# The ends of a stage, one transfer over two queues, and another order of feed-forward products in a two-layer encoder

## The chip, the core and the metric

The kernel runs on one core of a Trainium2 chip. The core has a matrix engine (PE, with its weight loader PEld), a vector engine (DVE), a scalar engine (ACT), a general engine (POOL), a queue for synchronisation and transfers (SP), and 16 DMA engines that all queues share. The metric is device time in microseconds of one execution. Before the change, three runs took 915.63, 916.13 and 916.91 us; the median is 916.13 us.

## The reference

The input x has 256 tokens of width 1024, in float32. Two layers follow, each made of a feed-forward part, an attention part and a second feed-forward part, and one last norm:

```python
for l in range(DEPTH):                                   # 2
    x = x + 0.5 * swiglu(rms_norm(x, n1[l]), wg1, wu1, wd1)   # hidden width 2816
    h = rms_norm(x, nm[l]); q, k, v = split(h @ w_in[l])
    out_a = windowed_gqa_sink(...)                       # 8 heads, window of 128
    out_b = differential_attention(...)                  # 4 heads, norm per head
    x = x + concat(out_a, out_b) @ w_out[l]
    x = x + 0.5 * swiglu(rms_norm(x, n2[l]), wg2, wu2, wd2)
return rms_norm(x, nf)

def swiglu(h, wg, wu, wd): return (silu(h @ wg) * (h @ wu)) @ wd
```

So there are four feed-forward parts; the text calls them parts 1 to 4, in order of time. Attention stands between parts 1 and 2 and between parts 3 and 4; part 3 follows part 2 directly.

## The kernel before

**Products.** Every float32 operand is split into a high part (a rounded copy, made by ACT) and a low part (the rest, made by DVE with a subtraction). A product of two matrices then takes three PE products: high with high, low with high, high with low. The 256 tokens are two blocks of 128; PE holds a block of x and streams 512 columns of weights. A feed-forward part takes its 2816 hidden columns in groups 0 to 4 of 512 and a last group of 256.

**Weights.** A step's weights are 1 MB, which come by DMA into one of six `raw` buffers (SP issues it), and are split in two halves into `w` buffers: for each half a cast on ACT and a subtraction on DVE. There are 14 `w` buffers, seven halves, so the splits run some three steps ahead of PE (`weights`, `ahead`, `emit_split`). A half's buffers are free again when PE has used it.

**The order of a part.** `order()` holds a list of names, which is worked off from left to right. Instructions keep the program's order on PE, ACT, DVE and POOL within a feed-forward part, so the list sets the order on each of them, and the order of the weights' transfers too. The names:

- `Pgp` is a quarter of an ordinary group g: p = 0, 1 are the two halves of the gate product, 2, 3 those of the up product; 24 PE products each (4 slices of x, 2 blocks, 3 products). After p = 1 ACT makes two silus, after p = 3 DVE makes the hidden values.
- Groups 2 and 4 are computed with seven half-size products instead of eight, by Strassen's way of adding operands first. `Sga`, `Sgd`, `Sgab`, `Sgc`, `Sgabc`, `Sgbc`, `Sgabcd` are these seven, 12 PE products each. The letters say which quarters of the weights have been added up. Sums are made by POOL with an accumulating DMA ("gather": b onto a, d onto a, c onto b) or by DVE ("plus": c onto a). Between them results are added up in bank `acc` and in `tmp` buffers: S2abc, S2bc and S2abcd all add into one PSUM bank, and DVE must have read it before the next of them starts.
- `x1` makes one of the four summed operands of x that the seven products need: DVE adds, ACT casts, DVE subtracts (`make_sums`).
- `F` turns the hidden values of a group: DVE transposes small blocks and SP issues four moves that put them in place (`Blocks`, `Flip`). `T` makes their high and low parts, on ACT and DVE. `Dgh` is the down product of group g for half h of the output columns, 24 products.
- `L0`, `L1` are the last group of 256; its turned values are `T5`. `A` stands for extra work: in part 1 the constants of attention (a small PE transpose, some small DVE work, one ACT exponential), in part 4 the final gain's load.

Part 1 to 4 all begin with 96 products of group 0, whose second half of slices needs x's second half. After the list come the last products of the part (`ffn_end`). They are: group 4's down products for output half 0; the tail (the last group's down product, which needs T5); group 3's remaining half (`late`); and output half 1.

**The end of parts 1 to 3** is `ffn_close`. For output half 0 it makes group 4's products of token block 0 (12), the tail of block 0 (6), adds the sum to x and, on DVE, transposes the new x (`closed`, `flip`), and then does the same for block 1. When both blocks are there, `flip` calls `move`, and SP issues four DMAs that finish turning x for the next stage; `flipped` makes x's operands from it. Output half 1 is turned in the same way at the end of part 2 and at the end of both attention parts (in `mix`). `Residual.late` makes those operands when the next stage has begun.

Of the kernel before, what the change touches and what calls it, by code (L numbers as in the profile page):

```python
# [32 lines left out]

def order():

    names = """P10 x1 S2a S2d x1 P11 x1 P12 T0 P13 x1 S2ab D00 S2c D01 S2abc P30 F1 S2bc P31 S2abcd T1 S4a P32 D10 P33 S4d T2 S4ab L0 F3 S4c D20 S4abc D21 T3 S4bc D11 S4abcd L1 D30 T4 T5 A"""
    out = []
    for n in names.split():
        what, g, rest = n[0], n[1:2], n[2:]
        if what == "x":  # L40
            out.append(("sums", 0, int(g)))
        elif what == "S":
            out.append(("seven", int(g), rest))
        elif what == "P":
            out.append(("plain", int(g), (int(rest) // 2, int(rest) % 2 * 4)))
        elif what == "D":
            out.append(("down", int(g), int(rest)))
        elif what == "L":
            out.append(("last", 0, int(g) * 4))
        elif what == "T":  # L50
            out.append(("turned", int(g), 0))
        elif what == "F":
            out.append(("flip", int(g), 0))
        elif what == "A":
            out.append(("aside", 0, 0))
    return out


ORDER = order()
GATHER = {"a": "b", "abc": "d"}  # L60
HELD = ("c", "abc")
# [3 lines left out]
def trunk(ctx: ExitStack, tc: tile.TileContext, x, n1, g1, u1, d1, nm, w_in, sink,  # L65
          lq1, lk1, lq2, lk2, subln, w_out, n2, g2, u2, d2, nf, out):
    nc = tc.nc
    sp = nc.sync
# [18 lines left out]
    pe, act, dve, pool = Kept(nc.tensor), Kept(nc.scalar), Kept(nc.vector), Kept(nc.gpsimd)  # L87
# [157 lines left out]
    def ahead(n):  # L245

        n = min(n, 2 * len(specs) - 1)
        while True:
            if at["split"] <= n and at["prep"] > at["split"] // 2:
                for _ in emit_split(*divmod(at["split"], 2)):  # L250
                    pass
                at["split"] += 1
            elif at["prep"] <= min(n // 2 + 1, len(specs) - 1) and at["dma"] > at["prep"] and \
                    (specs[at["prep"]].prep is None or at["split"] >= 2 * at["prep"]):
                prep = specs[at["prep"]].prep or []
                for todo in prep if isinstance(prep, list) else [prep]:
                    todo()
                at["prep"] += 1
            elif at["dma"] < min(at["use"] + AHEAD, len(specs)) and (specs[at["dma"]].moves is None or len(raws) < N_RAW):
                if specs[at["dma"]].moves is not None:  # L260
                    for _ in emit_dma(at["dma"]):
                        pass
                at["dma"] += 1
            else:
                break

    def weights(less=0, held=False):

        i = at["use"]
        at["use"] += 1  # L270
        if i > 1:
            ahead(2 * i + HALVES - less)
        w = loaded[i]
        w.held = held
        return w
# [58 lines left out]
    class Blocks:  # L334
# [7 lines left out]
            sq = self.sq.rearrange("p (g t m) -> p t g m", g=4, t=2)[:, t]  # L342
            dve.transpose(sq, src.rearrange("p (c i g) -> p g c i", i=32, g=4))

        def move(self):
            to = self.back.rearrange("p (b m) -> p b m", b=4)
            if not self.by_block:
                to = self.back.rearrange("p (t b m) -> p b t m", t=2, b=4)
            for b in range(4):
                sp.dma_start(to[:, b], self.sq[32 * b:32 * b + 32])  # L350

        def turned(self):
            if not self.by_block:
# [6 lines left out]
    class Norm:  # L360
# [21 lines left out]
        def flip(self, h, t):  # L382

            if h not in self.flips:
                self.flips[h] = Blocks(by_block=False)
            self.flips[h].take(xk[:, t, h * 512:h * 512 + 512], t)
            if t:
                self.flips[h].move()

        def flipped(self, h, js=(0, 1)):  # L390
            sl = self.flips[h].turned()
# [240 lines left out]
    class Residual:  # L632
# [14 lines left out]
        def late(self, k):  # L647

            if k == 1:
                if 1 in self.nxt.flips:  # L650
                    self.nxt.flipped(1)
                else:
                    self.nxt.pair(2)
                    self.nxt.pair(3)
                self.squares(1)
            elif k == 2:
                self.nxt.stats()
                self.nxt.copies()
# [180 lines left out]
    def ffn_end(parts, last):  # L839

        accs, hT, rest, late = parts
        hT = [None] * (2 * (NGRP - 1)) + hT
        hE = []
        w = {0: weights()}

        def group(h, order, a=None, c=slice(None), first=0):
            tokens(a or accs[h], hT, w[h], G4, first=first, last=last[h], order=order, cols=c)

        def tail(h, order=BY_TOKENS, a=None, c=slice(None)):
            if not hE:  # L850
                hE.extend(rest)
            tokens(a or accs[h], [None] * (2 * NGRP) + hE, w["rest"], 4 * NGRP, last=last[h], order=order, cols=c, h=h)

        return group, tail, late, w

    def ffn_close(parts, nxt, flips):
        group, tail, late, w = ffn_end(parts, (FC - 1, G4 + 3))
        res = Residual(nxt, parts[0])

        def closed(h, t):  # L860
            res.add(h, t)
            if h in flips:
                nxt.flip(h, t)

        group(0, [(k, 0) for k in range(4)])
        w["rest"] = weights()
        tail(0, [(k, 0) for k in range(2)])
        closed(0, 0)
        group(0, [(k, 1) for k in range(4)])
        tail(0, [(k, 1) for k in range(2)])  # L870
        closed(0, 1)
        late()
        w[1] = weights(2)
        tail(1)
        nxt.flipped(0)
        group(1, [(k, 0) for k in range(4)])
        ahead(2 * at["use"] - 2 + HALVES)
        closed(1, 0)
        group(1, [(k, 1) for k in range(4)])
        closed(1, 1)  # L880
        res.squares(0)
        nxt.late = res.late
# [242 lines left out]
    for l in range(DEPTH):  # L1125
        final = l == DEPTH - 1
        parts = ffn(norm, attention_constants, take_x) if l == 0 else ffn(norm)
        norm_m = Norm(16 + l * 8, False)
        ffn_close(parts, norm_m, (0,))
        norm2 = Norm(32 + l * 8)  # L1130
        mix(l, norm_m, norm2)
        parts = ffn(norm2, final_gain if final else None, final=final)
        if not final:
            norm = Norm((l + 1) * 8)
            ffn_close(parts, norm, (0, 1))
# [23 lines left out]
    group, tail, late, w = ffn_end(parts, ((FC - 1), FC - 1))  # L1159
# [50 lines left out]
```

## Time and profile before

One profiled execution took 918.63 us; its span is 916.8 us, at a mean granted clock of 0.998.

| | |
|---|---|
| median of three runs | 916.13 us |
| profiled execution, its span | 918.63 us, 916.8 us |
| PE busy | 899.1 us, 98% |
| DVE busy | 728.3 us, 79% |
| ACT busy | 559.0 us, 61% |
| bytes moved by DMA | 209.26 MB, mean 228 GB/s |
| DMA engines' share, first 7 of 40 slices | 90% or more |

How to read it: a timeline row has its start in us, its length in us, the engine, the operation, what it writes and reads (names without buffer numbers), the count of instructions merged in it, and in brackets how long the engine stood idle before it and what released it. `ps` is PSUM, `raw` and `w` are weights before and after splitting, `s` is a general buffer, `q` and `v` on PE rows are the summed operands. Queued work of SP and POOL has rows of its own (SPq is an issue, not the transfer). PE's products are pipelined, so that the end of a row overlaps the next.

### The profile page before, as it was taken

What the parts mean: (1) busy time and instruction counts of PE and PEld (TensorE: products, weight loads), DVE (VectorE), ACT (ScalarE), POOL (GpSimd) and SP (SyncE); (2) the same over time, 40 slices, a digit from 0 to 9 for tenths busy, and PEclk for the clock granted to TensorE, in tenths of its full rate; (3) what the DMA queues carried; (4) which work ended last, traced back from release to release, by engine and by line L of the source; (5) the groups of instructions that cost most, each with busy time, mean ns of one, the idle gap of its engine ahead of it and who ended that gap; (6) DMA issues with size and microseconds to landing.
All of it is one profiled execution on the core that took longest, in us unless ns stands there. A gap on an engine that the chain in (4) does not pass through costs nothing.

```text
span 916.8 us, 12682 instructions
## 1 busy us (share of the span) xinstructions
PE 899.1 (98%) x4540; PEld 756.2 (82%) x4540; DVE 728.3 (79%) x1098; ACT 559.0 (61%) x917; POOL 52.0 (6%) x73
## 2 busy tenths in 40 slices
PE   8999999999999999999999999999999999999997
PEld 6888788799888888888788888878997888888886
DVE  6687898779966788898668987977798668987982
ACT  6766566467754766666366665645676466665652
POOL 0400010000000000010000100000000000100001
PEclk9999999999999999999999999999999999999999
DMA  9999999666425779999669799996653449799931
GB/s 337 307 264 283 312 232 347 191 186 184 137 91 161 215 214 312 292 247 349 179 197 292 195 289 287 279 343 186 170 169 101 136 136 273 193 286 297 288 123 46
DMA packets 131247, 209.26 MB, mean 228 GB/s; under 512 B 5486, under 2 KB 51632, under 8 KB 131184
## 3 DMA queue, kind: packets, MB, share of 16 engines
q1 hardware_dynamic: 117168, 181.96, 59.6%
q0 software_dynamic: 12928, 25.46, 16.3%
q10 hardware_dynamic: 1088, 1.05, 0.3%
q8 instruction: 35, 0.57, 0.3%
q14 instruction: 28, 0.23, 0.1%
HBM read 192.71 MB, written 1.05 MB: 211 GB/s over the span
## 4 chain that ended last, share of the span: by engine, by line
PE 87%; DMA 5%; DVE 3%; issue 2%; ACT 0%; SPq 0%; POOL 0%; POOLq 0%; ACTq 0%; DVEq 0%
PE ps L80 87%; DVE s L80 2%; DMA s<-s 2%; DMA raw<-in_ffn_w_gate_dram 1%; DVE w L80 1%; DMA raw<-in_ffn_w_up_dram 1%; DMA raw<-in_w_in_dram 1%; DMA xk<-in_x_dram 0%; SPq L350 0%; ACT w L80 0%; POOL raw L80 0%; ACT s L80 0%; ACT tmp L80 0%; DVE ra L80 0%; DVE xk L80 0%
## 5 line engine op out<-in xcount | busy, mean ns | idle before, releaser
L80 PE MATMUL ps<-w,s 128*128 128x512 f32 (+1 forms) x2994 | 689.1, 390 | 5.1 <-ACT s L80 3.7
L80 PEld LDWEIGHTS ps<-w,s 128*128 128x128 f32 x2994 | 559.8, 188 | 122.8 <-ACT s L80 5.0
L80 DVE TENSOR_TENSOR w<-raw,w 128x1024 fp32r<-128x1024 f32 (+1 forms) x416 | 435.0, 1086 | 87.1 <-ACT w L80 83.0
L80 ACT CAST w<-raw 128x1024 fp32r<-128x1024 f32 (+1 forms) x416 | 375.1, 943 | 182.2 <-PE ps L80 114.3
L80 PE MATMUL ps<-s,w 128*128 128x256 f32 x672 | 84.0, 285 | 0.0
L80 PEld LDWEIGHTS ps<-s,w 128*128 128x128 f32 x672 | 81.7, 192 | 1.1
L80 PE MATMUL ps<-w,q 128*128 128x512 f32 x288 | 69.2, 389 | 0.0
L80 PEld LDWEIGHTS ps<-w,q 128*128 128x128 f32 x288 | 54.1, 188 | 11.2
L80 DVE STREAM_TRANSPOSE s<-s 128x512 f32<-128x512 f32 (+1 forms) x48 | 46.4, 1006 | 0.0
L80 DVE TENSOR_TENSOR s<-s,s 128x256 fp32r<-128x256 f32 x88 | 31.5, 419 | 15.0 <-ACT s L80 14.9
L80 ACT CAST s<-s 128x256 fp32r<-128x256 f32 x88 | 29.3, 402 | 14.8 <-DMA s<-s 14.8
L80 ACT ACTIVATE s<-s,negm 128x256 f32<-128x256 f32 x64 | 31.9, 500 | 8.7 <-DVE negm L80 8.7
L80 ACT ACTIVATE s<-s,gcol 128x256 fp32r<-128x256 f32 (+1 forms) x40 | 17.0, 500 | 31.6 <-DMA s<-s 31.6
L80 POOL DMA_DIRECT2D raw<-in_ffn_w_up_dram x16 | 20.7, 1297 | 256.9 <-DVE w L80 130.0
L80 ACT ACTIVATE tmp<-ps,r 128x512 f32<-128x512 f32 (+1 forms) x40 | 24.8, 643 | 12.4 <-PE ps L80 11.9
L80 ACT CAST q<-tmp 128x512 fp32r<-128x512 f32 x20 | 12.3, 616 | 28.5 <-DVE tmp L80 28.5
L80 DVE SCALAR_TENSOR_TENSOR s<-s,gcol,s 128x256 fp32r<-128x256 f32 x24 | 10.1, 483 | 20.7 <-ACT s L80 20.7
L80 PE MATMUL ps<-w,v 128*128 128x512 f32 x96 | 23.1, 389 | 0.0
L80 POOL TENSOR_TENSOR r<-ms,mhalf 128x2 f32<-128x2 f32 x6 | 4.3, 710 | 302.4 <-DVE ms L80 302.4
L80 PEld LDWEIGHTS ps<-w,v 128*128 128x128 f32 x96 | 18.0, 188 | 3.7
L80 DVE SCALAR_TENSOR_TENSOR s<-ps,hr,tmp 128x512 f32<-128x512 f32 (+1 forms) x32 | 20.4, 676 | 0.0
L80 DVE TENSOR_TENSOR q<-tmp,q 128x512 fp32r<-128x512 f32 x20 | 13.8, 689 | 8.3 <-ACT q L80 8.3
(112 smaller groups left out, 430.4 us busy)
## 6 DMA issues: line engine op xcount, KB each, us to landing
raw<-in_ffn_w_down_dram SPq DMA_DIRECT2D x44, 1024.0 KB, 9.0
raw<-in_ffn_w_gate_dram SPq DMA_DIRECT2D x39, 1024.0 KB, 6.2
raw<-in_ffn_w_up_dram SPq DMA_DIRECT2D x39, 1024.0 KB, 7.9
raw<-in_ffn_w_up_dram POOLq DMA_DIRECT2D x16, 1024.0 KB, 9.4
raw<-in_w_in_dram SPq DMA_DIRECT2D x14, 1024.0 KB, 7.7
s<-s SPq DMA_DIRECT2D x104, 128.0 KB, 4.7
raw<-in_ffn_w_gate_dram POOLq DMA_DIRECT2D x8, 1024.0 KB, 10.0
raw<-in_ffn_w_gate_dram SPq DMA_DIRECT2D x8, 512.0 KB, 4.4
```

What stands on the lines that cost most here:

```text
L80: ins = issue(*a, **k)
```

## The change

Three things are changed.

1. In `ffn_close`, group 4's products of both blocks for output half 0 come first, 24 in a row. Then come the tail of block 0, its closing, the tail of block 1, its closing.
2. `move` takes a list of queues and deals its four DMAs to them in turn. x's second half is moved by SP and ACT, two DMAs each; its first half and all hidden groups by SP alone as before.
3. The list in `order()` is another. S2a stands before P10. T0 stands before P11 and the fourth x1 before P12. S2c follows S2ab directly, D00 comes after it, D01 after S2bc. F1 comes later. In the second half S4ab, S4c and S4abc follow one another. T3 comes later, and A stands between T4 and T5. The steps themselves are the same.

```diff
-    names = """P10 x1 S2a S2d x1 P11 x1 P12 T0 P13 x1 S2ab D00 S2c D01 S2abc P30 F1 S2bc P31 S2abcd T1 S4a P32 D10 P33 S4d T2 S4ab L0 F3 S4c D20 S4abc D21 T3 S4bc D11 S4abcd L1 D30 T4 T5 A"""
+    names = """S2a x1 P10 x1 S2d x1 T0 P11 x1 P12 P13 S2ab S2c D00 S2abc P30 S2bc D01 P31 F1 S2abcd S4a P32 T1 P33 T2 D10 F3 S4d D20 S4ab S4c S4abc L0 S4bc D21 D11 T3 S4abcd L1 D30 T4 A T5"""
...
-        def move(self):
+        def move(self, queues=(sp,)):
...
-                sp.dma_start(to[:, b], self.sq[32 * b:32 * b + 32])
+                queues[b % len(queues)].dma_start(to[:, b], self.sq[32 * b:32 * b + 32])
...
-                self.flips[h].move()
+                self.flips[h].move((sp, act) if h else (sp,))
...
-        group(0, [(k, 0) for k in range(4)])
+        group(0, [(k, t) for t in range(2) for k in range(4)])
         w["rest"] = weights()
-        tail(0, [(k, 0) for k in range(2)])
-        closed(0, 0)
-        group(0, [(k, 1) for k in range(4)])
-        tail(0, [(k, 1) for k in range(2)])
-        closed(0, 1)
+        for t in range(2):
+            tail(0, [(k, t) for k in range(2)])
+            closed(0, t)
         late()
```

## The prediction

> **What bounds the kernel now.** I read the page's busy shares first, then the timeline of PE alone for the places where its row of products breaks off, then the timeline of all engines around those places, then DVE's timeline in the first third of a feed-forward part, because DVE prepares the weights of every product.
>
> ```profile
> PE 899.1 (98%) x4540; PEld 756.2 (82%) x4540; DVE 728.3 (79%) x1098; ACT 559.0 (61%) x917; POOL 52.0 (6%) x73
> ```
>
> PE is busy 98% of the span, and the granted clock of the run is 0.998. No product is added or taken away, so the change can only act on the breaks in PE's row. These are the ones it can touch:
>
> ```profile
> 83.26 2.88 PE L80 MATMUL ps<-w,q 128*128 128x512 f32 x12
> 85.98 5.60 PE L80 MATMUL ps<-w,s 128*128 128x512 f32 x24
> 93.07 24.73 PE L80 MATMUL ps<-w,s 128*128 128x512 f32 x108 [1.48 <-DVE tmp L80]
> ...
> 144.84 19.20 PE L80 MATMUL ps<-w,s 128*128 128x512 f32 x84
> ...
> 164.45 3.25 PE L80 MATMUL ps<-w,s 128*128 128x512 f32 x12 [0.24 <-ACT s L80]
> 168.21 19.61 PE L80 MATMUL ps<-w,s 128*128 128x512 f32 x84 [0.51 <-ACT s L80]
> ...
> 418.84 21.92 PE L80 MATMUL ps<-w,s 128*128 128x512 f32 x96
> 442.56 68.60 PE L80 MATMUL ps<-w,s 128*128 128x512 f32 x300 [1.79 <-ACT s L80]
> ...
> 595.32 21.98 PE L80 MATMUL ps<-w,s 128*128 128x512 f32 x96
> 618.41 19.61 PE L80 MATMUL ps<-w,s 128*128 128x512 f32 x84 [1.12 <-ACT s L80]
> ```
>
> Twelve products run from 83.26 to 85.98: 2.72 us, 0.2267 us for one. With that rate a break is start to start less the products between. At 168.21 PE lost 168.21 - 164.45 - 12 x 0.2267 = 1.04 us; at 442.56 it lost 442.56 - 418.84 - 96 x 0.2267 = 1.96; at 618.41, 1.33; at 93.07, 93.07 - 85.98 - 24 x 0.2267 = 1.65. The first three are the ends of parts 1, 2 and 3: PE stands before the tail, whose operands (T5) come last by a move through DMA. The fourth is in part 1: S2abcd waits for DVE to read S2bc's bank.
>
> **Stage ends.** At each end the 12 products of group 4 with block 1 now stand before the tail: 12 x 0.2267 = 2.72 us of work, for breaks of 1.04, 1.96 and 1.33. A second short wait comes right behind each, since the tail's second product needs the low part:
>
> ```profile
> 443.01 7.17 PEld L80 LDWEIGHTS ps<-w,s 128*128 128x128 f32 x32 [0.27 <-DVE s L80]
> ```
>
> With 0.27 each the needs are 1.31, 2.23 and 1.60, all under 2.72; the cover is left with 0.5 at the tightest. Gain 5.1. If a landing came 0.5 us later than now, part 2 would give the excess back.
>
> ```profile
> 625.10 0.68 DVE L80 TENSOR_TENSOR xk<-xk,ps 128x512 f32<-128x512 f32 x1
> 625.81 1.09 DVE L80 STREAM_TRANSPOSE s<-xk 128x512 f32<-128x512 f32 x1
> ...
> 633.93 1.71 ACT L80 ACTIVATE s<-s,gcol 128x256 fp32r<-128x256 f32 x4 [3.20 <-DMA s<-s]
> ...
> 637.86 3.04 PE L80 MATMUL ps<-s,w 128*128 128x256 f32 x24
> ```
>
> What is late next is x's first half, here at the end of part 3. Its block 0 is added and transposed only 6 products (1.36 us) before block 1, where it was 18 before. One add and one transpose take 625.81 - 625.10 = 0.71 and about 1.0, 1.7 us, so block 1 starts some 0.35 late and so do its four moves. The operands made from them begin at 633.93 and PE uses them at 637.86, so 0.35 costs nothing there. In part 1 the constants' work on DVE now stands ahead of T5's low parts:
>
> ```profile
> 168.87 0.19 DVE L80 COPY gcol<-ps 128x34 f32<-128x34 f32 x1
> ...
> 171.99 3.48 DVE L80 TENSOR_TENSOR w<-raw,w 128x1024 fp32r<-128x1024 f32 x3
> ```
>
> That is 3.1 us, which can begin once group 4's low parts are made, about 166; PE wants T5's at 164.45 + 5.44 = 169.9. It just fits, and I keep that end's 1.3 us as uncertain.
>
> **x's second half over two queues.** SP issues four moves one behind the other:
>
> ```profile
> 290.29 2.67 SPq L350 DMA_DIRECT2D s<-s  x4
> ...
> 295.20 1.71 ACT L80 ACTIVATE s<-s,gcol 128x256 fp32r<-128x256 f32 x4 [7.01 <-DMA s<-s]
> ...
> 290.30:291.30 1.00, 1.00 (x6) 0.82 (x5) 1.00 (x1) 0.00 (x0) 0.00 (x0) 1.00 0.00 0
> ...
> 290.30:295.30 5.00, 5.00 (x23) 4.13 (x22) 1.02 (x1) 0.10 (x1) 0.00 (x0) 1.00 0.53 105
> ```
>
> (The last two rows are stretches of 1 and of 5 us; their last but one figure is the DMA engines' share.) PE has no break here, so nothing is gained at the place itself. But ACT stood 7.01 us for the landing, and from there it works without a break up to the part's first gates, so parts 2, 3 and 4 start that much earlier on ACT and DVE. How much: two issues fewer in a row are 2 x 0.65 = 1.3 us at most; zero at least, as no move is issued later than now. The moves keep the 16 DMA engines busy for 0.53 x 5 = 2.65 us of the 4.9 from first issue to landing, and the first 1.0 passes before anything moves, so 1.0 + 2.65 and some 0.4 for the last landing is the floor, 4.1 instead of 4.9: I take 0.8, the end that the DMA engines' row gives. The Trainium skill, "DMA: Bandwidth & Descriptors", section "Issuing engines are not separate DMA queues", says that queues of several engines share the same 16 DMA engines and save only the issuing time; by it the gain would be the whole issue time of 1.3, no wait would be left in parts 2 and 4, and the sum would be 0.4 us lower. The trace agrees that SP's issues are spaced out; that they alone set the landing no row here shows.
>
> The cost: two issues of about 0.65 us on ACT, and a wait there for DVE's second transpose. Behind it on ACT stand the squares of x's first half and one weight cast, 2.6 us together; they fit into the 7.01 us. DVE's subtraction of that weight comes later too, but PE needs the weight two steps on. Cost nothing; if the idle time were gone, 1.3 us for each of the three places.
>
> **The order.** Steps and their products are the same. What changes is what DVE has done when PE comes to a step. DVE and ACT run in the order of the list, so I add up DVE's rows. Part 2, before:
>
> ```profile
> 317.40 0.70 DVE L80 TENSOR_TENSOR tmp<-s,s 128x512 f32<-128x512 f32 x1
> 318.78 0.69 DVE L80 TENSOR_TENSOR q<-tmp,q 128x512 fp32r<-128x512 f32 x1 [0.69 <-ACT q L80]
> 319.74 4.74 DVE L80 TENSOR_TENSOR w<-raw,w 128x1024 fp32r<-128x1024 f32 x4 [0.26 <-ACT w L80]
> 324.39 0.68 DVE L80 TENSOR_TENSOR tmp<-ps,tmp 128x512 f32<-128x512 f32 x1
> 324.99 0.68 DVE L80 SCALAR_TENSOR_TENSOR tmp<-tmp,s 128x512 f32<-128x512 f32 x1
> ...
> 334.20 1.43 DVE L80 TENSOR_TENSOR s<-s,s 128x256 fp32r<-128x256 f32 x4
> 335.54 2.35 DVE L80 TENSOR_TENSOR w<-raw,w 128x1024 fp32r<-128x1024 f32 x2
> 337.81 1.40 DVE L80 SCALAR_TENSOR_TENSOR s<-ps,hr,tmp 128x512 f32<-128x512 f32 x2
> ...
> 343.73 2.35 DVE L80 TENSOR_TENSOR raw<-raw,raw 128x1024 f32<-128x1024 f32 x2
> ```
>
> Start to start: an x1 takes 2.34 (317.40 to 319.74, two thirds work, the rest waits for ACT), a step's two weight subtractions 2.31 (4.65 for four), S2d's add 0.60, T0 1.34, "plus" (c onto a) 2.35, the hidden product of group 1 1.32. Test of the sum: from 317.40 to that hidden product stand three x1, five pairs, S2d's add and T0: 7.0 + 11.6 + 0.6 + 1.3 = 20.5, and the row is at 337.81, 20.41 later. DVE is the bound of this stretch, and it is behind PE:
>
> ```profile
> 334.52 2.88 PE L80 MATMUL ps<-w,q 128*128 128x512 f32 x12
> ...
> 511.00 2.88 PE L80 MATMUL ps<-w,q 128*128 128x512 f32 x12
> 513.17 1.40 DVE L80 SCALAR_TENSOR_TENSOR s<-ps,hr,tmp 128x512 f32<-128x512 f32 x2
> ...
> 784.73 2.88 PE L80 MATMUL ps<-w,q 128*128 128x512 f32 x12
> 788.03 1.40 DVE L80 SCALAR_TENSOR_TENSOR s<-ps,hr,tmp 128x512 f32<-128x512 f32 x2
> ```
>
> PE begins S2ab at 334.52 when P13 has ended; DVE takes P13's result 3.3 us later in part 2, 3.3 in part 4, 2.2 in part 3 (for part 1 I assume part 2's). After the change four x1 and "plus" come before that hidden product, and S2c, S2abc and S2bc follow sooner. The first place where PE must wait is S2bc, which adds into the bank that DVE reads for S2abc. DVE from 317.40 to that read's end: four x1 9.35, nine pairs (P12, P13, S2ab, S2c, D00, S2abc, P30, S2bc, D01) 20.8, two adds 1.2, T0 1.34, plus 2.35, hidden 1.32, the read 0.68: 37.0, so 354.4. PE: S2ab, S2c, D00, S2abc and P30 are 84 products, 19.04 us, so S2bc at 353.56. Wait 0.9 and a semaphore, 1.0 us. On the way the margins are thin: S2c's first weights are ready at 336.8 by the same sum (four x1, three pairs and a half, one add, T0) and PE wants them at 337.2, S2abc's at 345.1 against 345.4. Part 1 pays 1.0; parts 2 and 4 have 0.8 from the two queues and pay 0.2 each; part 3 starts 1.1 better and pays none. Together 1.4.
>
> Part 1 gains the break at 93.07. S2d's gate half is gathered onto the sum by POOL after S2abc's split:
>
> ```profile
> 73.10 1.27 POOL L80 DMA_DIRECT2D raw<-in_ffn_w_gate_dram  x1 [12.13 <-DVE w L80]
> ...
> 85.75 5.80 ACT L80 CAST w<-raw 128x1024 fp32r<-128x1024 f32 x6 [8.26 <-DMA raw<-in_ffn_w_gate_dram]
> ```
>
> ACT stood 8.26 us for it, and DVE's read of S2bc stood behind. In the new order S2abc's split ends some 2.4 us earlier by the sum above, and two steps (D01, P31; 10.9 us) instead of one stand between S2bc and S2abcd. Gain 1.65. The three steps of 12 products in a row later on (S4ab, S4c, S4abc) use weights at 2.72 us each, against 2.31 of DVE for a pair; DVE has caught up by then and I give them nothing, up to 1 us for each part.
>
> **Sum.** -5.1 - 1.65 + 1.4 = -5.35 us on the profiled execution, whose own time is 918.63 (span 916.8): 913.3. It lies 2.5 above the median of the runs, 916.13; the same difference gives 910.8, and I say 911.
>
> **Rivals.** (1) ACT becomes the bound of DVE's stretch. T0's four casts and group 1's gates take 1.3 us each on ACT:
>
> ```profile
> 328.14 1.25 ACT L80 ACTIVATE tmp<-ps,r 128x512 f32<-128x512 f32 x2
> ...
> 332.74 1.33 ACT L80 CAST s<-s 128x256 fp32r<-128x256 f32 x4
> ```
>
> They now stand between the x1 and the weight casts; if they come in series with DVE's rows, every part waits 2.6 us longer, 3.6 + 2.8 + 2.0 + 2.8 = 11.2 instead of 1.4, and the time is 916.1 - 6.75 + 11.2 = 920.6: slower. It decides from 6.75 / 4 = 1.7 us a part. For it: the 0.4 us of margin at S2c. Against: the sum of DVE's rows hit 337.81 within 0.1 with T0 in it. (2) The two queues bring nothing, since the DMA engines have no room for them together: parts 2 and 4 pay 1.0 each, 912.4, still faster. (3) The breaks at the ends only move: x's operands come late instead, by the whole 5.1. Then -0.25, no change, 915.9. Against: the 2 us of room ahead of 637.86. (4) DVE keeps up everywhere: no new wait, 909.4.
>
> **Chances.** The forecast as it stands 0.45, (2) 0.15, (4) 0.10: faster 0.70. (3) and mixtures near zero: 0.10. (1) and what else makes a part wait over 1.7 us: 0.20. What a measurement here tells from no change is 0.2%, 1.8 us. The likeliest case alone reaches from 909.5 to 913.5 (part 1's end given back, a step's pair more or less in DVE's sum); the range from 909 to 918.5 takes in (2), (3) and the lower half of (1).
>
> **What would show it.** After: PE runs from the last D30 product through the tail without a break in parts 2 and 3; the break before S2abcd in part 1 is gone; a break of about 1 us with DVE as releaser stands before the third pass of group 2 in part 1, and hardly one in parts 2 and 4; group 1's hidden product is taken some 7 to 8 us after P13's end instead of 3.3; ACT's wait for x's second half lands about 0.8 us earlier. Wrong if PE waits before P12, S2c or S2abc in several parts, or if the tails still wait.

## The result, and the profile after

The changed kernel takes 910.59 us (median of four runs, 910.35 to 910.97), the kernel before 916.52 us (median of four runs beside it, 915.63 to 917.28): a ratio of 0.9936, with a 95% interval of 0.9919 to 0.9953. The forecast was 911.0 us, faster. The profiled execution took 910.61 us; its span is 908.8 us, against 916.8 before.

The page's busy shares of the changed kernel:

```profile
PE 896.6 (99%) x4540; PEld 755.2 (83%) x4540; DVE 728.7 (80%) x1098; ACT 560.8 (62%) x917; POOL 53.1 (6%) x73
```

The same work stands in a shorter span. Where PE waited is in the view of PE's waits (what it wrote, what it waited for; us in total, times, longest). Before:

```profile
PE ps L80 <- ACT s L80: 3.7, 4, 1.8
...
PE ps L80 <- DVE tmp L80: 1.5, 1, 1.5
...
PE ps L80 <- DMA xk<-in_x_dram: 1.3, 2, 1.0
```

After:

```profile
PE ps L80 <- DVE s L80: 1.3, 2, 0.7
PE ps L80 <- DMA xk<-in_x_dram: 0.7, 2, 0.4
```

The wait for the turned operands ("ACT s") and the one before S2abcd ("DVE tmp") are gone; what DVE still causes ("DVE s") lies in attention and was there before too. A third, smaller difference is the kernel's very start ("DMA xk"), where nothing was changed.

For the sizes, PE's timeline of the kernel before needs two more rows beside those of the prediction, the start of S2ab in part 1 and the first attention product:

```profile
58.78 2.88 PE L80 MATMUL ps<-w,q 128*128 128x512 f32 x12
...
187.66 1.59 PE L80 MATMUL ps<-s,w 128*128 128x256 f32 x12
```

PE's timeline after, from S2ab of part 1 on:

```profile
57.83 2.88 PE L80 MATMUL ps<-w,q 128*128 128x512 f32 x12
...
80.04 40.96 PE L80 MATMUL ps<-w,s 128*128 128x512 f32 x180
...
137.16 24.64 PE L80 MATMUL ps<-w,s 128*128 128x512 f32 x108
...
183.80 3.04 PE L80 MATMUL ps<-s,w 128*128 128x256 f32 x24
...
409.55 95.36 PE L80 MATMUL ps<-w,s 128*128 128x512 f32 x420
504.75 2.88 PE L80 MATMUL ps<-w,q 128*128 128x512 f32 x12
...
583.63 46.40 PE L80 MATMUL ps<-w,s 128*128 128x512 f32 x204
629.87 3.04 PE L80 MATMUL ps<-s,w 128*128 128x256 f32 x24
```

In parts 2 and 3 PE now runs 420 and 204 products in one row, through the tail and into the next stage. In part 1, the 96 products from S2ab to the end of S2bc lie between 57.83 and 80.04, and the row from there on, with D01, P31 and S2abcd, has no break; in the old order 144 products lie between the start of S2ab at 58.78 and that of S2abcd at 93.07. With 0.2267 us for a product, start to start less the products between:

| stretch | lost before | lost after | gain |
|---|---|---|---|
| end of part 1 (144.84 to 187.66; 137.16 to 183.80) | 2.01 | 0.39 | 1.6 |
| end of part 2 (418.84 to 511.00; 409.55 to 504.75) | 2.39 | 0.00 | 2.4 |
| end of part 3 (595.32 to 637.86; 583.63 to 629.87) | 1.73 | 0.00 | 1.7 |
| part 1, from S2ab up to S2abcd (58.78 to 93.07; 57.83 to 80.04, nothing lost behind it) | 1.65 | 0.45 | 1.2 |
| up to S2ab of part 1 (58.78; 57.83) | | | 0.95 |

Together 7.9 of the 8.0 us between the two profiles. The medians are only 5.9 apart. The last two lines of the table, 2.15 us, are about the difference, and the experiments show that both vary from execution to execution.

### The profile page after: what moved, and what is told of

Same layout as the page of the kernel before. It is cut to its first block, busy times and chain, and to the rows that moved or that the text cites. A ratio compares the mean times of both kernels' runs of the same rounds, so it can differ in the third digit from the quotient of the medians.

```text
span 908.8 us, 12651 instructions
## 1 busy us (share of the span) xinstructions
PE 896.6 (99%) x4540; PEld 755.2 (83%) x4540; DVE 728.7 (80%) x1098; ACT 560.8 (62%) x917; POOL 53.1 (6%) x73
## 4 chain that ended last, share of the span: by engine, by line
PE 96%; DVE 2%; DMA 1%; issue 1%; ACT 0%; SPq 0%; POOLq 0%; POOL 0%; DVEq 0%
PE ps L80 96%; DVE s L80 2%; DMA raw<-in_ffn_w_gate_dram 1%; DVE w L80 1%; SPq L189 0%; ACT tmp L80 0%; DVE ra L80 0%; DVE xk L80 0%; ACT w L80 0%; POOLq L1203 0%; POOL rf L80 0%; DVE es L80 0%; SPq L482 0%; DVE rf L80 0%; DVE negm L80 0%
## 5 line engine op out<-in xcount | busy, mean ns | idle before, releaser
L80 ACT ACTIVATE junk<-xk 128x512 f32<-128x512 f32 x24 | 15.2, 631 | 19.0 <-issue 18.6
L80 ACT ACTIVATE tmp<-tmp,r 128x512 f32<-128x512 f32 x8 | 5.8, 725 | 26.2 <-DVE tmp L80 26.2
```

Of the source, the lines that this page charges most:

```text
L80: ins = issue(*a, **k)
```

## The experiments

The time of the kernel before wandered more between runs than that of the changed one, so each kernel was timed in five rounds together with the kernel before.

### The three edits, one by one

The first kernel has the new `ffn_close` alone.

```diff
-        group(0, [(k, 0) for k in range(4)])
+        group(0, [(k, t) for t in range(2) for k in range(4)])
...
+        for t in range(2):
+            tail(0, [(k, t) for k in range(2)])
+            closed(0, t)
```

> Only the ends are changed (group 4's products of both blocks first). The prediction's own sum: 916.5 - 5.1 = 911.4 us; PE goes through the tails of parts 1, 2 and 3 without a break, and T5's landing keeps its old time (5.1 to 5.3 us from its first issue). Rival: the old order made the late T5, the new order alone removes most of the breaks, so that ends and order overlap; then this kernel still gains about 5, but the order without it must gain nearly as much. A second rival, that breaks only move to x's first half: 916.5.

It took 913.01 us (11 runs, 911.66 to 915.71), ratio 0.9951 (0.9934 to 0.9968): 4.4 us less than the 917.42 of the kernel before beside it. The mechanism is right, the cover isn't always enough. Part 3 of its profile (SP's issues of T4's and T5's moves, ACT's casts of what they bring, PE):

```profile
600.34 2.80 SPq L350 DMA_DIRECT2D s<-s  x4
...
604.43 3.86 SPq L350 DMA_DIRECT2D s<-s  x4
```

```profile
608.69 1.33 ACT L80 CAST s<-s 128x256 fp32r<-128x256 f32 x4 [2.90 <-DMA s<-s]
612.45 0.71 ACT L80 CAST s<-s 128x256 fp32r<-128x256 f32 x2 [2.44 <-DMA s<-s]
```

```profile
609.14 21.15 PE L80 MATMUL ps<-w,s 128*128 128x512 f32 x91 [1.50 <-ACT s L80]
```

Here T4, which group 4's products need, came 8.35 us after its first issue, and PE waited 1.5 us before the products that were to be the cover. T5 came 8.0 us after its own. Neither landing took the 5.1 to 5.3 us that the expectation calls T5's "old time"; that figure was the changed kernel's, and the kernel before had 6.7 to 7.3.

The second kernel has x's second half on two queues alone.

```diff
-                self.flips[h].move()
+                self.flips[h].move((sp, act) if h else (sp,))
```

> Only x's second half is moved by SP and ACT, the rest is as before. Theory from the trace of the changed kernel: the operands of x's second half start 0.2 us earlier and PE has no break there, so no change, 916.5 within 0.5 us. The prediction's size, 0.8 us earlier, would also give no change in the time, but DVE would take the hidden product of group 1 in parts 2 and 4 about 0.8 us earlier against PE. Rival: ACT's two issues and its wait hold up weight casts, 0.5 to 1.3 us for each of three places, 918 to 920.

It took 919.04 us (12 runs, 914.22 to 922.32), ratio 1.0002 (0.9976 to 1.0029): no change, to within some 2.5 us either way. ACT's two issues and its first operands, at the start of part 2 of this kernel:

```profile
289.22 1.89 ACTq L80 DMA_DIRECT2D s<-s  x2
...
294.05 1.71 ACT L80 ACTIVATE s<-s,gcol 128x256 fp32r<-128x256 f32 x4 [0.48 <-DMA s<-s]
```

In the changed kernel, with DVE's subtractions behind them:

```profile
286.37 1.90 ACTq L80 DMA_DIRECT2D s<-s  x2
...
291.16 1.71 ACT L80 ACTIVATE s<-s,gcol 128x256 fp32r<-128x256 f32 x4 [0.42 <-DMA s<-s]
291.91 1.67 DVE L80 SCALAR_TENSOR_TENSOR s<-s,gcol,s 128x256 fp32r<-128x256 f32 x4
```

From the first issue to ACT's operands it is 4.83 and 4.79 us, against 290.29 to 295.20 = 4.91 before. The issuing did get shorter (1.9 us instead of 2.67), the landing hardly. ACT's work also moved: its squares and a cast now run in the wait (7.01 us idle before, 0.42 after), as the prediction said, and cost nothing.

The profile of this kernel shows something else. Its list is the old one, and in part 1 PE's timeline around S2abcd reads:

```profile
85.17 30.47 PE L80 MATMUL ps<-w,s 128*128 128x512 f32 x132
```

One row of 132 products; the break of 1.65 us that stood there before (at 93.07) isn't there. Nor is it in the four other profiles with the old first half (the kernel with the new ends alone and three kernels below: fewer bytes, F3 earlier, second half alone). It was an event of one execution of six. The start varies in the same way: in these six profiles, with the same code ahead of it, S2ab begins at 57.67 to 59.55, and at 58.78 in the kernel before.

The third kernel has the new list alone (the names are in the diff above).

> Only the list of order() is changed. The prediction's sum: +1.4 or more for new waits before S2bc (three places without the two queues: 1.0 + 1.0 + 1.0), -1.65 for S2abcd in part 1, the breaks at the three ends stay: 916 to 918. Theory from the trace of the changed kernel, where T5's transposing moves are issued earlier against PE: the breaks at the ends of parts 2 and 3 fall to 0 to 0.3 us by the order alone, that of part 1 to about 1.0, S2abcd gives 1.2: 911.0 to 912.0.

It took 913.24 us (10 runs, 912.46 to 913.85), ratio 0.9946 (0.9926 to 0.9966): as much as the ends alone, and far from the 916 to 918 of the prediction's sum. The fourth has ends and list, and x's second half on SP.

> The changed kernel with x's second half on SP alone: ends and order, without the two queues. The prediction: the two queues are worth 0.6 to 0.8 us in each of parts 2 and 4, so 910.6 + 1.6 = 912.2. Theory from the trace: they bring the landing 0.2 us forward, and DVE's read of S2abc keeps 1.0 us of margin, so no difference: 910.6 within 0.4 us.

910.64 us (6 runs, 910.51 to 911.38), ratio 0.9925 (0.9901 to 0.9948), and no break at any of the three ends. So the two queues are worth nothing that these runs show, and the two other edits overlap: 4.4 and 4.2 us alone, 6.8 together. On top of the new list the new ends bring 2.6. The profile of the list alone agrees: its three ends (137.40 to 185.23, 410.96 to 507.02, 585.90 to 632.75) still lose 1.6, 0.85 and 0.6, 3.0 in all, against 6.1 before.

### Why the list shortens the ends

The ends' breaks are waits for T5. T5's time from SP's first issue to ACT's cast, in parts 1, 2 and 3 of each profile (the last four kernels come further down):

| kernel | second half of the list | us |
|---|---|---|
| before | old | 6.9, 7.3, 6.7 |
| ends alone | old | 6.0, 5.9, 8.0 |
| two queues alone | old | 8.1, 8.1, 7.3 |
| list alone | new | 5.3, 5.2, 5.5 |
| ends and list | new | 5.2, 4.9, 6.2 |
| changed kernel | new | 5.1, 5.1, 5.3 |
| first half of the list alone | old | 6.7, 5.2, 6.1 |
| the same, F1 at its old place | old | 6.0, 7.9, 6.9 |
| second half of the list alone | new | 5.0, 7.1, 4.9 |
| changed kernel, more work for DVE | new | 5.1, 5.4, 5.0 |

The new second half mostly brings T5 in sooner, with one exception each way (7.1 with the new, 5.2 with the old). The first issue itself stands at the same place against PE, about 2.4 us after L1's last product. In part 2, SP's issues of the weights and of T5's moves, ACT's cast of T5, and the stretch from ten to five us before the first issue (its last but one figure is the DMA engines' share); before:

```profile
410.43 6.22 SPq L186 DMA_DIRECT2D raw<-in_ffn_w_down_dram  x4
...
434.83 3.30 SPq L350 DMA_DIRECT2D s<-s  x4
```

```profile
442.10 0.71 ACT L80 CAST s<-s 128x256 fp32r<-128x256 f32 x2 [3.98 <-DMA s<-s]
```

```profile
424.83:429.83 5.00, 5.00 (x24) 4.14 (x23) 4.35 (x5) 3.30 (x5) 0.00 (x0) 1.00 1.04 371
```

After:

```profile
398.14 13.84 SPq L186 DMA_DIRECT2D raw<-in_ffn_w_down_dram  x5
...
430.97 2.51 SPq L350 DMA_DIRECT2D s<-s  x4
```

```profile
436.06 0.71 ACT L80 CAST s<-s 128x256 fp32r<-128x256 f32 x2 [2.50 <-DMA s<-s]
```

```profile
420.97:425.97 5.00, 5.00 (x24) 4.14 (x23) 4.71 (x7) 3.30 (x5) 0.00 (x0) 1.00 0.82 226
```

Before, four loads of weights of 1 MB leave 24 to 18 us before T5's moves, and the DMA engines are full until five us before these come. After, five loads leave 33 to 19 us before them, and the engines have some room in that stretch. In the last five us ahead of the moves the share isn't lower after (0.91 before, 0.97 after), so only the earlier stretch tells the two apart. If the loads ahead are the cause, T5 must come sooner in the old list too when fewer bytes are loaded there. This kernel leaves out half of the bytes of four loads in each part, and so a part of the sums in its result.

```diff
-            if i > 1:
+            if i in cut:
+                sp.dma_start(dst[:, :2], src[:, :2])
+            elif i > 1:
...
-            raw = raw[:, 2 * j:2 * j + 2]
+            raw = raw[:, 0:2] if i in cut else raw[:, 2 * j:2 * j + 2]
```

> The kernel before, with only half of the bytes (512 KB) loaded for four steps of each part: D30, the two halves of group 4's down product and group 3's last; the second half of their slices uses the first half's weights, so that part of the products is left out of the result, and all instructions but the four loads stay. Theory: T5's moves are late because the DMA engines are still working off loads of weights; with 2 MB less, T5 lands about 5 to 5.5 us after its first issue instead of 6 to 8 and the breaks of parts 1, 2 and 3 fall to 0 to 0.4 us each: 912 to 914, as the new list alone gave. Rival: the landing is slow for another reason (SP's issues, the moves' own packets): 6 to 8 us still, 916.5 to 917.5.

It took 912.35 us (5 runs, 911.33 to 913.36), ratio 0.9959 (0.9944 to 0.9975). Part 2 of its profile:

```profile
432.11 2.53 SPq L357 DMA_DIRECT2D s<-s  x4
```

```profile
437.24 0.71 ACT L80 CAST s<-s 128x256 fp32r<-128x256 f32 x2 [2.55 <-DMA s<-s]
```

```profile
422.11:427.11 5.00, 5.00 (x24) 4.14 (x23) 4.36 (x5) 3.30 (x5) 0.00 (x0) 1.00 0.83 264
```

```profile
416.11 90.12 PE L80 MATMUL ps<-w,s 128*128 128x512 f32 x396
506.07 2.88 PE L80 MATMUL ps<-w,q 128*128 128x512 f32 x12
```

T5 lands after 5.1 us (5.5 and 5.4 in parts 1 and 3), and 396 products take 89.96 us where they took 92.16: with the old list and the old ends, 0.19 us of the 2.39 is left. So less traffic of weights ahead of T5 makes it land sooner. That this is all of it isn't shown. In the kernel with the second half of the list alone (its time is below; the profiled execution is its slowest, 916.84 us) the share in the stretch from ten to five us before T5's moves of part 2 is 0.81, the five loads leave 33 to 19 us before them, and T5, first issued at 433.46, still took 7.1 us and stopped PE:

```profile
440.51 0.71 ACT L80 CAST s<-s 128x256 fp32r<-128x256 f32 x2 [4.48 <-DMA s<-s]
```

```profile
440.96 4.26 PE L80 MATMUL ps<-w,s 128*128 128x512 f32 x11 [1.59 <-ACT s L80]
```

With the first half alone T5 took 5.2 us in part 2, with a share of 1.00 in that stretch. The Trainium skill, "DMA: Bandwidth & Descriptors", section "Queues, rings and completion order", says that each queue has one ring on every DMA engine and that its descriptors are taken in the order of the ring. The rows are in line with it, since T5's moves stand on SP's queue behind SP's loads, but they don't show that the ring is what delays T5: no run here put T5's moves on another queue.

Which name of the list does it? The first guess was F3, whose four moves took 5.09 us on SP in part 2, right ahead of the four loads.

```diff
-... P33 S4d T2 S4ab L0 F3 S4c D20 ...
+... P33 S4d T2 F3 S4ab L0 S4c D20 ...
```

> One name of the old list is moved: F3 from behind L0 to ahead of S4ab. In the old order SP's four moves of F3 take 5.1 us at 405 us of part 2 and four weight loads of 1 MB stand behind them on SP; they leave together some 24 us before T5's moves and the DMA engines are still at a share of 1.05 when these come. Theory: with F3 earlier the four loads leave up to 8 us earlier, the share in the 5 us before T5's moves falls under 0.9, T5 lands 5 to 5.5 us after its first issue, and most of the ends' breaks go: about 913.5 to 914.5 (part 1 keeps none of the constants' delay). Rival: the loads wait for free raw buffers and not for F3's moves; they leave at the same time, T5 takes 6 to 8 us, 916.5.

The guess was wrong: 925.33 us (6 runs, 920.13 to 927.28), ratio 1.0099 (1.0069 to 1.0129). The loads did begin earlier (the first at 404.64), now ahead of S4abcd's accumulating gather and not behind it. POOL's issue of that gather and ACT's wait for what it brings, in part 2:

```profile
407.33 1.28 POOL L80 DMA_DIRECT2D raw<-in_ffn_w_gate_dram  x1 [14.17 <-DVE w L80]
```

```profile
420.80 2.00 ACT L80 CAST w<-raw 128x1024 fp32r<-128x1024 f32 x2 [8.05 <-DMA raw<-in_ffn_w_gate_dram]
```

ACT had what it brings 13.5 us after its issue; the splits, the buffers and the next loads all came late behind it, and T5, first issued at 439.81, took 7.3 us. The counter-test puts F3 back in the new list.

```diff
-... D10 F3 S4d D20 S4ab S4c S4abc L0 S4bc ...
+... D10 S4d D20 S4ab S4c S4abc L0 F3 S4bc ...
```

> The new list alone, with F3 put back behind L0 (old ends, one queue). Compared with the new list alone, 913.2. Theory: F3's moves, standing ahead of the next weight loads on SP, hold these back until shortly before T5's moves; T5 lands 6 to 8 us after its first issue again and the breaks at the ends of parts 1, 2 and 3 return, 916 to 917. Rival: what matters is that S4ab, S4c and S4abc stand together, so that the gather of S4abcd and the loads behind it leave earlier; then T5 still lands after 5.0 to 5.5 us and the time stays within 0.7 us of 913.2.

912.56 us (7 runs, 912.46 to 913.78), ratio 0.9966 (0.9954 to 0.9978); T5 after 5.4, 5.2 and 6.4 us. F3's place isn't it. In this kernel, as in the changed one, S4abcd's gather is issued 35 us before T5's moves in part 2 (396.69 to 431.68), and four of the five loads leave before F3; in the old list it is 31 us (403.48 to 434.83), and the four loads leave behind F3. What else of the second half is needed (S4c and S4abc together, S4d later, D21 behind S4bc) wasn't taken apart and stays open.

### The halves of the list

> Only the second half of the list is new (after S2abcd). Theory: all that the order gained alone (916.5 to 913.2) comes from here, through T5's landing, which falls from 6 to 8 us to about 5.2 us after its first issue: 913.2 within 0.6 us. Rival: the first half has a part in it, then this stays at 914.5 to 916.

The new second half alone, in the old kernel, took 912.52 us (12 runs, 911.85 to 916.84), ratio 0.9965 (0.9948 to 0.9983): all that the list is worth. The first half alone:

> Only the first half of the list is new (up to S2abcd, S2d's other place included); the second half and everything else as before. The prediction: 1.65 us gained before S2abcd in part 1, 1.0 us lost before S2bc in each of parts 1, 2 and 4, so 917. Theory after the first four runs: the break before S2abcd stood in one profile of the old order and in neither of the two others of it, and DVE keeps up, so no change, 916.5 within 1 us, and T5's landing stays long (6 to 8 us from its first issue).

923.58 us (6 runs, 921.26 to 930.24), ratio 1.0108 (1.0073 to 1.0143), against the expectation. The cut itself made a wait: the new first half has F1 behind P31, the old second half begins with T1. ACT's cast of T1 and PE's products with it, in part 1:

```profile
103.93 1.32 ACT L80 CAST s<-s 128x256 fp32r<-128x256 f32 x4 [8.94 <-DMA s<-s]
```

```profile
104.38 15.56 PE L80 MATMUL ps<-w,s 128*128 128x512 f32 x60 [1.96 <-ACT s L80]
```

ACT, whose order is fixed, stands 8.9 us at T1, and the casts of weights stand behind it. With F1 left at its old place the wait should go.

```diff
-... P30 S2bc D01 P31 F1 S2abcd | T1 S4a P32 ...
+... P30 F1 S2bc D01 P31 S2abcd | T1 S4a P32 ...
```

> The first half of the list is new but for F1, which keeps its old place behind P30; the second half is old. With F1 behind P31 and T1 at its old place directly behind S2abcd, PE had waited 0.8 to 2.0 us for T1 in three parts and the time was 923.6. Theory: that wait was made by the cut through the list; with F1 two steps earlier it goes, and the first half alone is worth nothing, 917 within 1.2 us. The prediction: -1.65 and + 3 x 1.0, 918.5. Rival: the first half costs by itself even so, 920 or more.

916.99 us (12 runs, 914.01 to 919.66), ratio 1.0009 (0.9994 to 1.0023). The first half of the new list is worth nothing by itself. F1's later place needs T1's later place; T1's later place alone costs nothing, as the second half alone shows.

### DVE's margin

The prediction had DVE's sum decide whether the list costs. In the changed kernel DVE's timeline of part 2 (first x1, group 1's hidden product, read of S2abc) and PE's row of S2bc are:

```profile
313.35 0.70 DVE L80 TENSOR_TENSOR tmp<-s,s 128x512 f32<-128x512 f32 x1
...
338.16 1.41 DVE L80 SCALAR_TENSOR_TENSOR s<-ps,hr,tmp 128x512 f32<-128x512 f32 x2
...
348.02 0.69 DVE L80 TENSOR_TENSOR tmp<-tmp,ps 128x512 f32<-128x512 f32 x1
```

```profile
349.71 2.88 PE L80 MATMUL ps<-w,q 128*128 128x512 f32 x12
```

The read ends at 348.71, 1.0 us before PE comes to S2bc. To see whether that margin is real, four more instructions were put in DVE's way.

```diff
                 dve.tensor_tensor(sm[:, :, P:S], v, f(sm[:, :, 0:P]), op=ALU.subtract)
+                dve.tensor_tensor(sm[:, :, P:S], v, f(sm[:, :, 0:P]), op=ALU.subtract)
```

> The changed kernel, with the last subtraction of each x1 done twice: four more DVE instructions of 0.60 to 0.69 us in each part ahead of S2ab's weights, 2.4 to 2.8 us. Theory from the trace of the changed kernel (DVE's read of S2abc ends 1.0 us before S2bc in parts 2 and 4, 2.6 in part 3, level with it in part 1): waits of about 1.6 in parts 2 and 4, 0 in part 3, 2.6 in part 1, so 910.6 + 5.8 = 916.4. The prediction's sum, with no margin in parts 2 and 4 and a wait of 1.0 in part 1: + 2.6 in parts 1, 2 and 4 and + 2.5 in part 3, 920.9. Rival, that DVE's chain isn't near the bound: 910.6.

914.15 us (12 runs, 913.87 to 914.61), 3.6 more than the changed kernel and 2.2 less than the theory had it. By part, PE lost 1.9 us more in part 1, 0.9 in part 2, 0.9 in part 4 and nothing in part 3. In part 2 the two ends of DVE's stretch are now:

```profile
315.25 0.67 DVE L80 TENSOR_TENSOR tmp<-s,s 128x512 f32<-128x512 f32 x1
...
351.52 0.67 DVE L80 TENSOR_TENSOR tmp<-tmp,ps 128x512 f32<-128x512 f32 x1
```

The four instructions cost DVE 1.6 us and not 2.4 to 2.8 (36.27 instead of 34.67), since the 0.26 us that DVE had waited for ACT after an x1 were now filled. So 1.6 us of DVE made a wait of 0.9 in parts 2 and 4: the margin there is some 0.7 us, in part 1 nil. About half of the wait appeared earlier than at S2bc, at S2c's weights, so the 1.0 us ahead of S2bc aren't what bounds the margin:

```profile
336.11 2.57 PE L80 MATMUL ps<-w,v 128*128 128x512 f32 x10 [0.23 <-DVE w L80]
```

### The constants ahead of T5

In the kernel with the new list alone, the end of part 1 still has a break; PE's row, and DVE's work ahead of T5's low parts (first row of the constants, then T5):

```profile
162.15 3.24 PE L80 MATMUL ps<-w,s 128*128 128x512 f32 x13
166.28 19.11 PE L80 MATMUL ps<-w,s 128*128 128x512 f32 x83 [0.90 <-DVE s L80]
```

```profile
162.70 0.18 DVE L80 COPY gcol<-ps 128x34 f32<-128x34 f32 x1
...
165.82 0.75 DVE L80 TENSOR_TENSOR s<-s,s 128x256 fp32r<-128x256 f32 x2
```

```diff
-... L1 D30 T4 A T5
+... L1 D30 T4 T5 A
```

> The new list alone, with T5 ahead of A as in the old one. Theory: the 1.2 us that PE still loses at the end of part 1 in the new list alone are the constants' work on DVE ahead of T5's low parts; with T5 first they go, 912.0 to 912.3. Rival: T5's landing sets that break and the constants only fill the time before it, 913.2.

911.80 us (5 runs, 911.61 to 912.13), ratio 0.9954 (0.9937 to 0.997), and the break is gone:

```profile
161.95 22.40 PE L80 MATMUL ps<-w,s 128*128 128x512 f32 x96
184.19 3.04 PE L80 MATMUL ps<-s,w 128*128 128x256 f32 x24
```

That end loses 0.48 us instead of 166.28 - 162.15 - 13 x 0.2267 = 1.18 at the break alone. The two ratios overlap; the runs (912.46 to 913.85 without, 911.61 to 912.13 with T5 first) don't, but weren't taken side by side. In the changed kernel the ends' 2.72 us cover the constants.

## Why the prediction was right

The time, 910.6, lies where the forecast had it, and the ends carry it. Two of the other terms, -1.65 and +1.4, were both wrong and cancelled, which was luck.

- **Stage ends, 5.1.** Right in size: 5.7 on the two profiles, and the mechanism given works, as the ends alone show. The rest is the small breaks behind the tail. What the step didn't see is that the breaks had a second cure: T5's landing had been taken as given by its 6.7 to 7.3 us, and less traffic ahead of it makes it shorter. The list alone takes 4.2, the ends alone 4.4, both 6.8, so not all that the step gave to the new ends is theirs: on top of the list they bring 2.6. The prediction's "if a landing came 0.5 us later" was the right worry: in the kernel with the ends alone T4 and T5 took over 8 us in part 3, and the cover was too small.
- **The break before S2abcd, 1.65.** Wrong as a term: it was a one-time event of the profiled execution. The step that failed is the transfer to the median: "2.5 above the median" may well have been this break (1.65) and the start (0.95 later than in the changed kernel), and the sum took the first of them off the median as well.
- **Waits at S2bc, 1.4.** Too much: none in parts 2, 3 and 4, 0.45 in small pieces in part 1, of which 77.22 - 71.61 - 24 x 0.2267 = 0.17 stand right before S2bc. The sum of DVE's rows gave 37.0 us from the first x1 to the read's end; it was 348.71 - 313.35 = 35.4. One of the two weight subtractions of D01's pair stands behind the read (1.1), a pair takes 2.27 instead of 2.31 (0.3), and T0 fills one x1's wait for ACT (0.3). The hidden product came 338.16 - 330.67 = 7.5 us after P13, within the forecast 7 to 8. That DVE is near the bound was right: 0.7 us of margin.
- **Two queues, 0.8 earlier.** Wrong: 0.1 us at ACT's operands and nothing at DVE's subtractions, which begin 5.5 us after the first issue in both (290.29 to 295.75 before, 286.37 to 291.91 after):

```profile
295.75 1.68 DVE L80 SCALAR_TENSOR_TENSOR s<-s,gcol,s 128x256 fp32r<-128x256 f32 x4 [4.43 <-ACT s L80]
```

 The first half of rival (2) was right, that the two queues bring nothing; its second half, waits of 1.0 in parts 2 and 4, wasn't, because the margin was there without them. Its reason, no room in the DMA engines, wasn't tested. The step that failed is the floor from the DMA engines' share; the 0.4 us for the last landing in it stands in no row, and 4.8 us passed where the floor had 4.1. The Trainium skill's rule that the prediction cites ("DMA: Bandwidth & Descriptors", "Issuing engines are not separate DMA queues") says that only issuing time is saved; the trace agrees with that as an upper bound, with 0.8 us of issuing saved and 0.1 us of time.
- **x's first half and ACT's issues at nothing.** Right: PE runs on through 504.75 and 629.87, and ACT's squares went into its idle time.
- **The constants ahead of T5, "just fits".** Right with the new ends (0.39 lost in all); without them they cost 1.2.
- **The rivals.** ACT didn't become the bound (1), the breaks didn't move (3). In (1)'s sum, part 3's 2.0 should by the prediction's own figures be 1.0 + 2.6 - 1.1 - 0.8 = 1.7, which changes nothing. (4), DVE keeps up, came true in three parts, but its time, 909.4, rested on the break before S2abcd.

Corrected, the sum on the medians is 5.7 for the ends, by both cures, and nothing for the rest: 916.5 - 5.7 = 910.8. The 5.7 comes from one pair of profiles; T5's landing varies from execution to execution, and the 5.7 with it. The ends and the list without the two queues reach the same time; nothing tried here went below it.

## What to carry to other kernels

A wait for a small move through DMA has two cures, work to cover it and less traffic ahead of it; find out how long the move takes where the DMA engines have room before pricing either, and don't add up what the two bring. A break that stands at one place of one profile is a term only if a second profile has it too; where the profile is slower than the median, the difference is likely made of just such breaks. When a list is cut for an experiment, look first at which pairs (F1 and T1 here) the cut tears apart.

## What the hardware showed that was not expected

- A move of 128 KB took 0.95 us of ACT's queue (1.90 for two), 0.67 of SP's. Two queues shortened the issuing by 0.8 us and the landing by 0.1: at least here the landing of four moves isn't set by how fast they are issued.
- The landing of T5's moves varied from 5.2 to 8.1 us in the five kernels of the table above with the old second half, from 4.9 to 7.1 in the five with the new; the middle values are 6.9 and 5.2.
- Whole runs took 914.46 to 923.39 us for the kernel before beside the first four kernels, 912.46 to 913.85 for the new list alone, 910.51 to 911.38 for ends and list. T5 is not the only thing that differs: the five longest of these runs of the kernel before (920.72 and more) show a granted clock of 0.994 to 0.997, its runs under 918 us 0.998 or 0.999. As an estimate, 0.4% of clock is 3.7 us of 917. Whether the breaks lower the clock, or the clock is a second cause of the longer time, no run here shows.
- S4abcd's accumulating gather of 1 MB took 13.4 us from issue to landing in part 2 of the kernel with F3 earlier, where a load of 1 MB left 2.7 us ahead of it and three more behind it. In the changed kernel, whose loads begin 2.0 us behind the gather (398.14 after 396.13), it took 9.8.
